# A decoder layer on one core: memory queries and two branch products as seven quarter products each

## The chip, the cores and the metric

One core of a Trainium2 chip runs the whole kernel. The metric is the device time in microseconds of one launch, the median of several runs. Products run on TensorE (PE), element-wise work on VectorE (DVE) and ScalarE (ACT); SyncE (SP) and GpSimd (POOL) issue the transfers. Inputs lie in the chip's memory (HBM), operands in on-chip memory (SBUF), sums of products in eight banks of PSUM.

## The reference

A decoder layer over 512 tokens of width 1024 in float32. One projection of the normed input gives the queries, keys and values of three attention branches and three gates; the branches are mixed, and a SwiGLU network follows.

```python
u = rms_norm(h, ln_mix_pre[l])
proj = jnp.einsum('bsd,de->bse', u, w_in[l])
qa, ka, va, qb, kb, vb, qm, gl = jnp.split(proj, split_idx, axis=-1)
y_swa = swa_sink_attention(...)          # 8 heads of 64, window of 128
y_sb = stick_breaking_attention(...)     # 8 heads of 64
y_mem = memory_cross_attention(...)      # 4 heads of 128, 256 memory positions
g = jax.nn.sigmoid(gl.reshape(B, S, N_BRANCH, D))
merged = (g[:, :, 0] * jnp.einsum('bse,ed->bsd', y_swa, w_branch_swa[l])
          + g[:, :, 1] * jnp.einsum('bse,ed->bsd', y_sb, w_branch_sb[l])
          + g[:, :, 2] * jnp.einsum('bse,ed->bsd', y_mem, w_branch_mem[l]))
mix = jnp.einsum('bsd,de->bse', merged, w_out[l])
h = h + rms_norm(mix, ln_mix_post[l])
u = rms_norm(h, ln_ffn_pre[l])
a = silu(u @ w_gate[l]) * (u @ w_up[l])
h = h + rms_norm(a @ w_down[l], ln_ffn_post[l])
```

The memory queries `qm` are 512 x 1024 by 1024 x 512. Each branch product is 512 x 512 by 512 x 1024.

## The kernel before, in words

Every float32 operand of a large product is split into a high and a low half (`split`: ScalarE rounds the high half, VectorE subtracts it for the low one), and `mm3` makes three products of them: high by high, high by low, low by high. A product works on a stationary block of 128 x 128 and a moving block of 128 rows by up to 512 columns.

The work is a stream of units (class `Stream`). Each unit loads 1024 columns of weights for each of the 128 partitions (512 KB), splits them, and makes its products; loads run four units ahead, splits three. Attention heads (`sb_head`, `swa_pair`, `mem_pair`) are written as steps between which the stream runs for a given number of microseconds (`dn.run`), so that TensorE has stream products while the other engines do the heads' softmax or scan.

The units in order: projections (`proj`), values, memory keys and values, three of the four memory-query projections, the stick-breaking branch (`add_branch(SB)`), the fourth memory query, and then for each branch SB, SWA (local attention) and MEM its gate units, with SWA's and MEM's branch units behind their gates.

- A projection unit for the queries of a memory head (`proj("qm", i)`) has 8 chunks of width 128, each with three products of 512 columns. The result is scaled by the norm of the row and split.
- A branch (`branch_t`) takes two units per half of the output columns. For each of 4 token tiles it multiplies 4 pieces of `y` by the weights, then gates: one multiplication by the gate, one addition to the sum of the branches so far.
- The gates are made as seven quarter products in place of eight, a Strassen scheme (Winograd's form): the input is cut into token halves and chunk halves, the weights into chunk halves and output halves. `QUART` names the seven products p1, p2, p5, p3, p6, p7, p4; each has two units. p1, p6, p7 and p4 add up in one PSUM bank, p5 and p3 in a second, p2 is a third (`QBANK`), and copies taken between them (`q_end`) are joined to the four quarters. Sums of weight quarters are made by loads that add into the buffer of an earlier product (`q_issue`: p1 to p5 to p6 to p4, p3 to p7), on POOL's queue; each such load has to follow the split of what was in the buffer. The sums of input quarters are `qsum`. The feed-forward products have the same form (`gu`, `down`).

`merge` transposes the gated sum of one half of the columns, for all tokens, and splits it; `mix_mm` multiplies it by `w_out`. At the end of the mixing phase the calls stand as: first half of tile 0, `merge(1)`, first half of tile 1, second half of tile 0, and so on.

The order of instructions on each engine is written out in a table (`ORDER`), and the buffer that each tile takes in another (`PLAN`; kinds are raw weights, high and low halves, PSUM banks `p`, the 73 SBUF blocks `ck`, small tiles `s`).

Of the kernel before, what the change touches and what calls it, by code (L numbers as in the profile page):

```python
# [17 lines left out]
P = 128  # L18
# [11 lines left out]
QM_FIRST = 3  # L30
# [11 lines left out]
    ),  # L42
    "vector": (
# [30 lines left out]
    ),  # L74
    "scalar": (
# [24 lines left out]
    ),  # L100
    "gpsimd": (
        "5-12 4 2-3 16 0 29 1 14 13 15 30 17 22 27 21 20 19 18 23 28 25 24 26 31-34 36-37 35 38 40 39 41-49 51 50 "
        "52-65 70 66 69 71 67-68 72-95 107-112 96-99 103 101 100 102 104-106"
    ),
    "sync": (
# [1799 lines left out]
```

## Time and profile before

| | |
|---|---|
| median of 3 runs | 783.92 us (783.35 to 784.14) |
| profiled execution, first to last instruction | 782.6 us |
| TensorE busy | 775.0 us, 99%, 4638 products |
| VectorE busy | 601.9 us, 77% |
| ScalarE busy | 472.9 us, 60% |
| GpSimd busy | 88.5 us, 11% |
| granted TensorE clock | 0.997 |
| bytes moved | 128.61 MB, mean 164 GB/s |

The profiled execution is one execution; its own time is given as the span between its first and last instruction, 1.3 us under the median, which counts the whole launch. A group row of the profile reads: line, engine, operation, out<-in, shapes, count | busy us, mean ns of one | idle time before it and who ended it. A timeline row reads: start, duration, engine, line, operation, out<-in, shapes, count. Almost all instructions have the line of one helper, so groups are told apart by tile names.

### The profile page before, as it was taken

The numbers are of one execution on the slowest core, as the hardware profiler recorded it, in microseconds if no ns is written. First come the engines' busy times: TensorE is split into PE (matmuls) and PEld (weight loads), VectorE is DVE, ScalarE is ACT, GpSimd is POOL, SyncE is SP. The second block draws the span as 40 slices with busy tenths as digits, with TensorE's granted clock in tenths as the row PEclk, the third lists the DMA queues.
The fourth block names the chain that finished last, engine by engine and source line by source line (L and its number), as shares of the span: only waits on it lengthen the run. The fifth ranks groups of instructions, "written<-read, shape, count | busy, mean of one in ns | idle before, by whom it ended". The sixth has DMA issues, their size and how long they took to land.

```text
span 782.6 us, 12274 instructions
## 1 busy us (share of the span) xinstructions
PE 775.0 (99%) x4638; PEld 682.9 (87%) x4638; DVE 601.9 (77%) x961; ACT 472.9 (60%) x843; POOL 88.5 (11%) x117
## 2 busy tenths in 40 slices
PE   9999999999999999999999999999999999999996
PEld 6889888778888888888888899999999999888885
DVE  7995787677886657976856699978677878999876
ACT  7652677677486657556644486545555447666753
POOL 2100400001012120011002101000000000216000
PEclk9999999999999999999999999999999999999998
DMA  8444923245559694379569638977777652959702
GB/s 302 129 142 121 315 90 109 81 126 143 109 118 205 166 189 131 82 190 231 210 240 282 110 105 225 235 190 189 183 182 183 180 159 78 198 128 195 216 1 108
DMA packets 44220, 128.61 MB, mean 164 GB/s; under 512 B 5248, under 2 KB 6832, under 8 KB 44160
## 3 DMA queue, kind: packets, MB, share of 16 engines
q1 hardware_dynamic: 30480, 85.21, 33.4%
q0 software_dynamic: 13248, 42.22, 29.0%
q8 instruction: 36, 0.59, 0.3%
q10 hardware_dynamic: 432, 0.39, 0.2%
q14 instruction: 24, 0.20, 0.1%
HBM read 120.98 MB, written 4.72 MB: 161 GB/s over the span
## 4 chain that ended last, share of the span: by engine, by line
PE 99%; DVE 0%; issue 0%; DVEq 0%; ACT 0%
PE p L185 99%; DVE fg L185 0%; DVEq L1893 0%; DVE s L185 0%; DVE wide L185 0%; ACT sqr L185 0%; DVE eps_t L185 0%
## 5 line engine op out<-in xcount | busy, mean ns | idle before, releaser
L185 DVE TENSOR_TENSOR lo<-raw,hi 128x1024 fp32r<-128x1024 f32 (+4 forms) x139 | 159.4, 1154 | 65.5 <-ACT hi L185 64.8
L185 ACT CAST hi<-raw 128x1024 fp32r<-128x1024 f32 (+4 forms) x139 | 137.5, 997 | 96.3 <-PE p L185 60.0
L185 DVE TENSOR_TENSOR lo<-wide,hi 128x1024 fp32r<-128x1024 f32 x53 | 64.8, 1224 | 22.5 <-ACT hi L185 21.9
L185 ACT CAST hi<-wide 128x1024 fp32r<-128x1024 f32 x53 | 55.6, 1052 | 38.6 <-PE p L185 17.8
L185 PE MATMUL p<-lo,lh 128*128 128x512 f32 x154 | 59.9, 389 | 0.0
L185 PE MATMUL p<-hi,ll 128*128 128x512 f32 x154 | 59.7, 389 | 0.0
L185 PE MATMUL p<-hi,lh 128*128 128x512 f32 x154 | 59.3, 389 | 0.0
L185 PE MATMUL p<-lo,uh 128*128 128x512 f32 (+1 forms) x160 | 57.1, 357 | 0.0
L185 PE MATMUL p<-hi,ul 128*128 128x512 f32 (+1 forms) x160 | 57.1, 357 | 0.0
L185 PE MATMUL p<-hi,uh 128*128 128x512 f32 (+1 forms) x160 | 56.9, 358 | 0.0
L185 PE MATMUL p<-uh,hi 128*128 128x512 f32 x136 | 55.3, 406 | 0.0
L185 PE MATMUL p<-uh,lo 128*128 128x512 f32 x136 | 53.3, 392 | 0.0
L185 PE MATMUL p<-ul,hi 128*128 128x512 f32 x136 | 53.2, 392 | 0.0
L185 POOL DMA_DIRECT2D wide<-in_w_gu x21 | 18.1, 876 | 186.1 <-DMA wide<-in_w_gu 185.7
L185 POOL DMA_DIRECT2D raw<-in_w_g x24 | 20.7, 861 | 135.8 <-DVE lo L185 128.8
L185 PEld LDWEIGHTS p<-lo,lh 128*128 128x128 f32 x154 | 28.9, 188 | 6.0
L185 PEld LDWEIGHTS p<-hi,lh 128*128 128x128 f32 x154 | 28.9, 188 | 6.0
L185 PEld LDWEIGHTS p<-hi,ll 128*128 128x128 f32 x154 | 28.9, 188 | 5.9
L185 PEld LDWEIGHTS p<-hi,uh 128*128 128x128 f32 x160 | 30.0, 188 | 4.0 <-issue 0.2
L185 PEld LDWEIGHTS p<-lo,uh 128*128 128x128 f32 x160 | 30.0, 188 | 3.7
L185 PEld LDWEIGHTS p<-hi,ul 128*128 128x128 f32 x160 | 30.0, 188 | 3.7
L185 ACT COPY gp<-p 128x512 f32<-128x512 f32 x33 | 19.3, 587 | 21.4 <-PE p L185 21.3
(645 smaller groups left out, 2390.0 us busy)
## 6 DMA issues: line engine op xcount, KB each, us to landing
wide<-in_w_gu SPq DMA_DIRECT2D x31, 512.0 KB, 5.1
raw<-in_w_gu SPq DMA_DIRECT2D x26, 512.0 KB, 5.3
raw<-in_w_g POOLq DMA_DIRECT2D x24, 512.0 KB, 5.9
wide<-in_w_gu POOLq DMA_DIRECT2D x21, 512.0 KB, 7.1
raw<-in_w_g SPq DMA_DIRECT2D x18, 512.0 KB, 4.4
raw<-in_w_p SPq DMA_DIRECT2D x14, 512.0 KB, 4.3
raw<-in_w_brt SPq DMA_DIRECT2D x12, 512.0 KB, 4.2
bp<-in_w_dn SPq DMA_DIRECT2D x22, 256.0 KB, 6.9
```

The costliest lines, as they stand in the source:

```text
L185: ins = f(*args, **kw)
```

## The change

Three products take the form that the gates have.

- **Memory queries.** The four `proj("qm", ...)` units go. Seven units `qm_quart` come, each with 2 heads x 4 chunks, three products of 256 columns (half of the tokens). They use the gates' sums of input quarters, so the result is not yet scaled by the row's norm; that scale goes into the softmax of the memory heads (`qscale`).
- **Branches SWA and MEM.** Their four units each go. Seven units `b_quart` come, each with 2 token tiles x 2 pieces, three products of 512 columns. `pair_out` keeps a plain copy of `y` (`yraw`), `y_sums` builds the sums of its quarters, `y_parts` splits them, `c_end` joins the banks and hands each finished tile to gating. For SWA the addition of the SB part becomes an adding transfer on POOL's queue.
- **Weights** of these units: p1, p2, p3 are plain loads by SP, p5, p6, p4 and p7 adding loads by POOL (`c_issue`), issued three units ahead of the earlier product's turn.
- **Order of units.** Query units alternate with the last two gate units of SB and the first five of SWA; SWA's branch units with the last four gate units of SWA, MEM's with the last four of MEM (`woven`).
- **Merging** goes by half of the columns and half of the tokens; the first tile is mixed in one go.
- **Tables.** `ORDER` and `PLAN` are new throughout, the opening and the feed-forward part included. Raw weights may take three further buffers inside the wide block (`kind in ("raw", "fraw") and n > 3`). In the list of PSUM banks the long run of the feed-forward units was `3 5 7 0 2 6 4 1 7 5 3 6 ...` and is `2 2 2 5 5 5 2 2 2 5 5 5 ...`.

```diff
-    def merge(h):
+    CHAIN = {"p5": "p1", "p6": "p5", "p4": "p6", "p7": "p3"}
+    def c_issue(b, p):
+        if p in CHAIN:
+            t = cw[(b, p)] = cw.pop((b, CHAIN[p]))
+            nc.gpsimd.dma_start(t[:, :].rearrange("p (c n) -> p c n", c=2), c_src(b, p), accum_op=ALU.add)
+            return
+        uid[0] += 1
+        t = cw[(b, p)] = places.take(wp, "raw", [P, 1024], F32, f"raw{uid[0]}")
+        nc.sync.dma_start(t[:, :].rearrange("p (c n) -> p c n", c=2), c_src(b, p))
+    def y_sums(b, k):
...
+        nc.vector.tensor_tensor(p5, ya[:, hi], yb[:, hi], op=ALU.subtract)
+        nc.vector.tensor_tensor(p6, p5, ya[:, lo], op=ALU.subtract)
+        nc.vector.tensor_tensor(p3, p6, yb[:, lo], op=ALU.add)
+        nc.vector.tensor_tensor(p7, ya[:, lo], ya[:, hi], op=ALU.subtract)
+    def c_end(b, p, i, put):
+        ps = cbank[(b, QBANK[p], i)]
+        if p in ("p1", "p5", "p6", "p7"):
+            t = ckeep[(b, p, i)] = ck(f"cq{b}{p}{i}")
+            nc.scalar.copy(t[:, :], ps[:, :])
+        if p == "p2":
+            t = ckeep.pop((b, "p1", i))
+            nc.vector.tensor_tensor(t[:, :], ps[:, :], t[:, :], op=ALU.add)
+            put(0, 0, t)
...
+        elif p == "p4":
+            put(1, 0, ps)
+    def b_quart(b, p):
+        def gen(hi, lo):
+            first = p in ("p1", "p5", "p2")
+            for i in range(2):
+                def put(half, h, v):
+                    t = 2 * half + i
+                    g = gate_t[(b, t, h)]
+                    nc.vector.tensor_tensor(g[:, :], v[:, :], g[:, :], op=ALU.mult)
+                    more = acc_t[(t, h)] if b == SWA else gate_t[(SWA, t, h)]
+                    if b == SWA:
+                        nc.gpsimd.dma_start(g[:, :], more[:, :], accum_op=ALU.add)
+                    else:
+                        nc.vector.tensor_tensor(g[:, :], g[:, :], more[:, :], op=ALU.add)
...
+                for k in range(2):
+                    mm3_behind(ps[:, :], b_left(b, p, k, i * P), cols((hi, lo), k * 512, 512), first and k == 0, k == 1)
+                yield 1.36
+                c_end(b, p, i, put)
+            if b == MEM and p in ("p3", "p7"):
+                merge(("p3", "p7").index(p), 0)
+    def qm_quart(p):
...
+            for f in range(2):
+                for k in range(4):
+                    x = q_left(p, k // 2, k % 2, 0, 256)
+                    w = cols((hi, lo), f * 512 + k * P, P)
+                    mm3(ps[:, f * 256 : (f + 1) * 256], w, x, first and f == 0 and k == 0, k == 3)
+                yield 1.44
+    sb, swa, mem = (gate_units(b) for b in (SB, SWA, MEM))
+    seq = sb[:12] + woven(branch_units("qm"), sb[12:] + swa[:5]) + swa[5:10]
+    seq += woven(branch_units(SWA), swa[10:])
+    seq += mem[:10] + woven(branch_units(MEM), mem[10:])
...
-        yield 3.0
+        yield 4.0
...
-    mix_mm(0, 0, 4)
-    merge(1)
-    mix_mm(1, 0, 4)
-    mix_mm(0, 4, KC)
+    mix_mm(0, 0, KC)
+    merge(1, 1)
     tmp[0] = mix(0)
-    mix_mm(1, 4, KC)
+    merge(0, 1)
+    mix_mm(1, 0, KC)
```

More of the change, by code (lines that the diff above doesn't have):

```diff
@@ L241, in take @@
             return pool.tile(shape, dt, tag=f"ck{n}", name=name, bufs=1)
-        if kind == "fraw" and n > 3:
+        if kind in ("raw", "fraw") and n > 3:
             return self.held["wide0"][:, (n - 4) * 1024 : (n - 3) * 1024]
@@ L652, in mem_vals @@
         return gen
-    merged = [None] * 8
+    merged = {}
     QUART = ("p1", "p2", "p5", "p3", "p6", "p7", "p4")
@@ L794, in gen @@
                 for k in range(2):
-                    mm3_behind(qbank[key][:, :], q_left(p, c, k, i), cols((hi, lo), k * 512, 512), first and k == 0, c == 1 and k == 1)
+                    mm3_behind(qbank[key][:, :], q_left(p, c, k, i * P), cols((hi, lo), k * 512, 512), first and k == 0, c == 1 and k == 1)
                 yield 1.36
@@ L810, in gen @@
                 tok = slice(t * P, (t + 1) * P)
-                ps = (aps if b == SB and t % 2 else dps)(f"br{b}{t}{h}")
+                ps = (aps if t % 2 else dps)(f"br{b}{t}{h}")
                 for k in range(4):
@@ L816, in gen @@
                     yield 0.68
-                if b == SB:
-                    acc_t[(t, h)] = ck(f"bs{t}{h}")
-                    with tc.high_priority():
-                        nc.vector.tensor_copy(acc_t[(t, h)][:, :], ps[:, :])
-                    continue
-                g = gate_t[(b, t, h)]
-                with tc.high_priority():
-                    nc.vector.tensor_tensor(g[:, :], ps[:, :], g[:, :], op=ALU.mult)
-                eng = nc.vector
-                more = acc_t[(t, h)] if b == SWA else gate_t[(SWA, t, h)]
@@ L827, in gen @@
-                eng.tensor_tensor(g[:, :], g[:, :], more[:, :], op=ALU.add)
-                if (b, h, t) == (MEM, 1, 1):
-                    merge(0)
-        return gen
-    def merge(h):
-        for c in range(4):
-            pt = (dps if (h, c) in ((1, 0), (1, 1)) else aps)(f"mg{h}{c}")
-            for t in range(NT):
-                nc.tensor.transpose(
-                    pt[:, t * P : (t + 1) * P], gate_t[(MEM, t, h)][:, c * P : (c + 1) * P], ident[:, :]
-                )
-            mh, ml = ck(f"mgh{h}{c}", F32R), ck(f"mgl{h}{c}", F32R)
-            split(pt[:, :], mh[:, :], ml[:, :])
-            merged[4 * h + c] = (mh, ml)
+                acc_t[(t, h)] = ck(f"bs{t}{h}")
@@ new lines, in c_got, with got @@
+    def c_got(b, p):
+        def got():
+            if p not in CHAIN:
+                c_issue(b, p)
+            return cw[(b, p)]
+        return got
+    def y_sums(b, k):
+        lo, hi = slice(0, 256), slice(256, 512)
+        sl = slice(k * 256, (k + 1) * 256)
+        ya, yb = yraw[(b, k)], yraw[(b, 2 + k)]
+        if k == 0:
+            for p in ("p5", "p6", "p3", "p7"):
+                ysum[(b, p)] = ck(f"ys{b}{p}")
+        p5, p6, p3, p7 = (ysum[(b, p)][:, sl] for p in ("p5", "p6", "p3", "p7"))
+        nc.vector.tensor_tensor(p5, ya[:, hi], yb[:, hi], op=ALU.subtract)
+        nc.vector.tensor_tensor(p6, p5, ya[:, lo], op=ALU.subtract)
+        nc.vector.tensor_tensor(p3, p6, yb[:, lo], op=ALU.add)
+        nc.vector.tensor_tensor(p7, ya[:, lo], ya[:, hi], op=ALU.subtract)
@@ new lines, in y_parts, with b_left @@
+    def y_parts(b, p):
+        ysum[(b, p)] = parts(f"yp{b}{p}", ysum[(b, p)])
+    def b_left(b, p, k, o):
+        if p in ("p1", "p2", "p4"):
+            return cols(y[(b, k if p == "p1" else 2 + k)], o + (256 if p == "p4" else 0), P)
+        return cols(ysum[(b, p)], k * 256 + o, P)
+    def c_end(b, p, i, put):
[7 more added lines that the diff above has]
+            put(0, 0, t)
+        elif p == "p6":
+            t = ckeep.pop((b, "p6", i))
+            nc.vector.tensor_tensor(t[:, :], cbank[(b, "y", i)][:, :], t[:, :], op=ALU.subtract)
+            put(0, 1, t)
+        elif p == "p7":
+            t, x = ckeep.pop((b, "p5", i)), ckeep.pop((b, "p7", i))
+            nc.vector.tensor_tensor(t[:, :], t[:, :], x[:, :], op=ALU.subtract)
+            put(1, 1, t)
+        elif p == "p4":
+            put(1, 0, ps)
@@ new lines, in b_quart @@
+    def b_quart(b, p):
[11 more added lines that the diff above has]
+                        nc.vector.tensor_tensor(g[:, :], g[:, :], more[:, :], op=ALU.add)
+                if first:
+                    cbank[(b, QBANK[p], i)] = (dps if p == "p2" else aps)(f"b{b}{p}{i}")
+                ps = cbank[(b, QBANK[p], i)]
+                for k in range(2):
[4 more added lines that the diff above has]
+                merge(("p3", "p7").index(p), 0)
+        return gen
@@ new lines, in qm_quart, with gen, put @@
+    def qm_quart(p):
+        def gen(hi, lo):
+            first = p in ("p1", "p5", "p2")
+            if first:
+                cbank[("qm", QBANK[p], 0)] = (dps if p == "p2" else aps)(f"q{p}")
+            ps = cbank[("qm", QBANK[p], 0)]
+            for f in range(2):
[4 more added lines that the diff above has]
+                yield 1.44
+            def put(half, h, v):
+                st[("qm", h, half)] = parts(f"qms{half}{h}", v)
+            c_end("qm", p, 0, put)
+        return gen
@@ new lines, in merge @@
+    def merge(h, half):
+        for c in range(2):
+            pt = aps(f"mg{h}{c}{half}")
+            for k in range(2):
+                for t in range(2):
+                    o = (2 * c + k) * P
+                    nc.tensor.transpose(
+                        pt[:, (2 * k + t) * P : (2 * k + t + 1) * P],
+                        gate_t[(MEM, 2 * half + t, h)][:, o : o + P],
+                        ident[:, :],
+                    )
+            merged[(h, c, half)] = parts(f"mg{h}{c}{half}", pt)
@@ L845, in tile_kernel, with merged_at @@
+    def merged_at(k, t):
+        return cols(merged[(k // 4, k % 4 // 2, t // 2)], (k % 2) * 256 + (t % 2) * P, P)
     for c in range(8):
@@ new lines, in add_quarters @@
+    def add_quarters(seq):
+        at = {}
+        for kind, b, p, c in seq:
+            at[(kind, b, p, c)] = len(dn.units)
+            if kind == "gate":
+                dn.add(q_got(b, p, c), 1024, quart(b, p, c))
+            else:
+                dn.add(c_got(b, p), 1024, qm_quart(p) if b == "qm" else b_quart(b, p))
+        for kind, b, p, c in seq:
+            if p in CHAIN:
+                u_begin = dn.units[at[(kind, b, CHAIN[p], c)] - (2 if kind == "gate" else 3)]["begin"]
+                if kind == "gate":
+                    u_begin.append(lambda b=b, p=p, c=c: q_issue(b, p, c))
+                else:
+                    u_begin.append(lambda b=b, p=p: c_issue(b, p))
+            if kind == "branch" and b != "qm":
+                n = at[(kind, b, p, c)]
+                if p == "p1":
+                    for k in range(2):
+                        dn.units[n - 2 + k]["begin"].append(lambda b=b, k=k: y_sums(b, k))
+                elif p not in ("p2", "p4"):
+                    dn.units[n - 2]["begin"].append(lambda b=b, p=p: y_parts(b, p))
+        return at
@@ new lines, in gate_units, with branch_units, woven @@
+    def gate_units(b, ps=QUART):
+        return [("gate", b, p, c) for p in ps for c in range(2)]
+    def branch_units(b, ps=QUART):
+        return [("branch", b, p, 0) for p in ps]
+    def woven(*rows):
+        out = []
+        rows = [list(r) for r in rows]
+        while any(rows):
+            for r in rows:
+                out += r[:1]
+                del r[:1]
+        return out
+    sb, swa, mem = (gate_units(b) for b in (SB, SWA, MEM))
+    seq = sb[:12] + woven(branch_units("qm"), sb[12:] + swa[:5]) + swa[5:10]
@@ new lines, in tile_kernel @@
+    seq += woven(branch_units(SWA), swa[10:])
+    seq += mem[:10] + woven(branch_units(MEM), mem[10:])
+    g0 = len(dn.units)
+    at = add_quarters(seq)
+    dn.units[at[("gate", SWA, "p4", 1)]]["flags"].append(f"gates{SWA}")
+    dn.units[at[("gate", MEM, "p2", 1)]]["flags"].append("gates_late")
+    dn.mark(f"branch{MEM}")
+    for g, what, f, args in (
+            (-8, "begin", x_quarters, (1, 1)),
+            (-8, "begin", x_quarters, (0, 1)),
+            (-7, "begin", x_quarters, (0, 0)),
+            (-6, "begin", x_quarters, (1, 0)),
+            (-6, "begin", q_sum1, (0,)),
+            (-5, "begin", q_sum1, (1,)),
+            (-4, "begin", q_sum2, ()),
+            (-3, "begin", q_gain, (1,)),
+            (-2, "begin", q_sum3, ()),
+            (-1, "begin", q_gain, (0,)),
+            (0, "begin", q_sum4, ()),
+            (1, "begin", q_parts, ("p5", 0)),
+            (2, "begin", q_parts, ("p5", 1)),
+            (3, "begin", q_parts, ("p3", 0)),
+            (4, "begin", q_parts, ("p3", 1)),
+            (5, "begin", q_parts, ("p6", 0)),
+            (6, "begin", q_parts, ("p6", 1)),
+            (7, "begin", q_parts, ("p7", 0)),
+            (8, "begin", q_parts, ("p7", 1)),
+        ):
+            dn.units[g0 + g][what].append(lambda f=f, args=args: f(*args))
@@ L1061, in pair_out @@
     def pair_out(b, c, ps):
+        if b != SB:
+            yraw[(b, c)] = ck(f"yr{b}{c}")
+            nc.scalar.copy(yraw[(b, c)][:, :], ps[:, :])
         y[(b, c)] = parts(f"y{b}{c}", ps)
@@ L1222, in mem_pair @@
                 )
-            nc.vector.tensor_scalar(nm, nm, -MS, None, op0=ALU.mult)
+            nc.vector.tensor_tensor(nm, nm, qscale[:, 4:], op=ALU.mult)
             for n in range(NT):
                 fn(
-                    blocks(w[h], n), blocks(s[h], n), AF.Exp, bias=nm[:, n : n + 1], scale=MS, accum_out=den[:, n : n + 1]
+                    blocks(w[h], n),
+                    blocks(s[h], n),
+                    AF.Exp,
+                    bias=nm[:, n : n + 1],
+                    scale=qscale[:, n : n + 1],
+                    accum_out=den[:, n : n + 1],
                 )
@@ L1320, in mix_mm @@
     def mix_mm(t, k0, k1):
-        tok = slice(t * P, (t + 1) * P)
         if k0 == 0:
```

96 lines of the change are left out of this document (31 added, 65 removed), and 183 rows, old and new, of tables (ORDER, PLAN).

## The prediction

> **What bounds the kernel now.** I read the page first: busy times, then the chain that ended last, then the list of waits of TensorE alone.
>
> ```profile
> span 782.6 us, 12274 instructions
> PE 775.0 (99%) x4638; PEld 682.9 (87%) x4638; DVE 601.9 (77%) x961; ACT 472.9 (60%) x843; POOL 88.5 (11%) x117
> PE 99%; DVE 0%; issue 0%; DVEq 0%; ACT 0%
> PE p L185 <- DVE wide L185: 1.4, 1, 1.4
> ```
>
> TensorE is busy for 99% of the span, the chain runs along it, and its only listed wait is 1.4 us at the start. So the kernel is as long as its list of products, each at the pace at which products follow one another. That pace is not the "mean ns of one" of a group, since neighbours overlap; it is the distance between starts:
>
> ```profile
> 308.00 0.39 PE L185 MATMUL p<-hi,y00h 128*128 128x512 f32 x1
> 310.72 0.39 PE L185 MATMUL p<-hi,y00h 128*128 128x512 f32 x1
> 561.98 0.28 PE L185 MATMUL p<-T3h,hi 128*128 128x256 f32 x1
> 564.86 0.28 PE L185 MATMUL p<-B21h,hi 128*128 128x256 f32 x1
> 51.73 0.31 PE L185 MATMUL p<-hi,uh 128*128 128x320 f32 x1
> 52.17 0.31 PE L185 MATMUL p<-hi,uh 128*128 128x320 f32 x1
> ```
>
> The first two are the same product of two token tiles, 12 products apart: 2.72/12 = 0.2267 us for 512 columns. The next two are 24 products apart: 2.88/24 = 0.1200 us for 256 columns. The last two, three apart, give 0.147 us for 320 columns.
>
> **The change part by part: TensorE.** These rows show the products that are replaced:
>
> ```profile
> L185 PE MATMUL p<-uh,hi 128*128 128x512 f32 x136 | 55.3, 406 | 0.0
> L185 PE MATMUL p<-hi,y10h 128*128 128x512 f32 x8 | 3.1, 390 | 0.0
> ```
>
> A projection unit is 8 chunks times 3 products (hi by hi, hi by lo, lo by hi), so 136 is 17 units, 4 of them memory queries. They go: 4 x 24 = 96 products, 96 x 0.2267 = 21.76 us. In come 7 quarters x 2 heads x 4 chunks x 3 = 168 products of 256 columns, 168 x 0.1200 = 20.16 us. Gain 1.60 us.
> In a branch, each left piece (y10h and so on) meets 2 halves x 4 tiles = 8 times; 4 pieces x 8 x 3 = 96 products. After: 7 x 2 x 2 x 3 = 84, of the same 512 columns. Gain 12 x 0.2267 = 2.72 us for local attention, the same for memory, 5.44 us.
> The transposes of the merge stay 32, the scores of the memory heads stay as they are. Together **-7.04 us** of TensorE.
>
> **VectorE.** Its pace, too, is the distance of starts:
>
> ```profile
> 386.70 0.69 DVE L185 TENSOR_TENSOR wo14l<-wo,wo14h 128x512 fp32r<-128x512 f32 x1
> 387.31 0.69 DVE L185 TENSOR_TENSOR wo05l<-wo,wo05h 128x512 fp32r<-128x512 f32 x1
> 569.72 1.23 DVE L185 TENSOR_TENSOR lo<-raw,hi 128x1024 fp32r<-128x1024 f32 x1 [0.23 <-ACT hi L185]
> 570.86 0.42 DVE L185 TENSOR_TENSOR aq<-gp,sg 128x256 f32<-128x256 f32 x1
> 571.20 1.22 DVE L185 TENSOR_TENSOR raw<-raw,raw 128x1024 f32<-128x1024 f32 x1
> ```
>
> That is 0.61 us for 512 elements, 1.14 for 1024, 0.34 for 256. The memory branch adds 3 splits of weights (3.4), 8 sums of y quarters (2.7), 4 splits of these sums (2.4) and 6 joins of banks (3.7): +12.2 us. Local attention adds the same and gives its 8 adds (4.9) to DMAs: +7.3. The queries add 3 splits and lose one evacuation net: +2.8. In all +22.3, so 624 of some 775 us, 81%. On average that is cover enough; in the last stretch it is not plenty. Where that stretch lies today, and the fullest stretches elsewhere:
>
> ```profile
> 300.00:342.00 42.00, 42.00 (x226) 36.17 (x225) 36.03 (x67) 24.98 (x57) 1.72 (x2) 1.00 0.37 93
> 342.00:404.00 62.00, 62.00 (x284) 51.54 (x283) 43.55 (x57) 35.73 (x53) 5.16 (x6) 1.00 0.77 214
> 342.00:382.00 40.00, 40.00 (x179) 33.10 (x178) 25.97 (x30) 29.18 (x42) 5.16 (x6) 1.00 0.94 252
> 448.00:476.00 28.00, 28.00 (x235) 27.88 (x234) 26.88 (x49) 21.88 (x46) 1.72 (x2) 1.00 0.44 111
> 672.00:756.00 84.00, 84.00 (x373) 69.53 (x372) 75.68 (x119) 56.74 (x96) 17.47 (x21) 1.00 0.71 161
> ```
>
> Columns: stretch, PE, PEld, DVE, ACT and POOL busy, clock, DMA share, GB/s. From 300 to 404 us (both branches, memory heads, memory gates) VectorE works 79.6 of 104 us. After, the same work needs 79.6 + 12.2 + 7.3, and the four last units of the local gates are woven in (4 splits and 2 joins, 5.8): **105 us of VectorE work beside 104 - 5.4 + 4 x 2.72 = 109.4 us of products, 96%**. At 448 to 476 us VectorE is at 26.88/28 = 96% and TensorE lost nothing; at 672 to 756 it is at 90% for 84 us, again without loss. So it can be covered, with nothing to spare. The scaling of the memory maxima changes its operand, not its count.
>
> **ScalarE** gets 45 instructions more (9 splits, 20 copies out of PSUM, 8 splits of sums, 8 copies of y):
>
> ```profile
> L185 ACT CAST hi<-raw 128x1024 fp32r<-128x1024 f32 x120 | 125.5, 1053 | 85.1 <-PE p L185 54.8 <-DVE raw L185 16.7 <-issue 8.6
> L185 ACT COPY gp<-p 128x512 f32<-128x512 f32 x33 | 19.3, 587 | 21.4 <-PE p L185 21.3
> ```
>
> At most 9 x 1.05 + 36 x 0.6 = 31 us, 504 of 775: hidden, since today it idles 40%.
>
> **DMA.** SP issues 3 loads fewer (3 x 3 raw quarters for 3 x 4 halves); POOL issues 12 accumulating loads and 8 adds of 256 KB more, on the queue that also carries the gates' accumulations.
>
> ```profile
> q1 hardware_dynamic: 30480, 85.21, 33.4%
> q0 software_dynamic: 13248, 42.22, 29.0%
> raw<-in_w_g POOLq DMA_DIRECT2D x24, 512.0 KB, 5.9
> xq<-xq POOLq DMA_DIRECT2D x8, 256.0 KB, 5.3
> DMA to landing us min/median/max: 2.6/5.2/17.1
> ```
>
> By the first two rows 512 KB take 1.61 us of all 16 engines on q1 (33.4% of 782.6 over 85.21 MB) and 2.82 on q0. So +12 x 2.82 + 8 x 1.41 - 3 x 1.61 = +40 us. For the stretch above: 0.37 x 42 + 0.77 x 62 = 63 today; plus two branches (2 x 9.7), the adds (11.3) and four gate units (9.2) makes 103 of 109 us, 94%. The row 342 to 382 shows that share for 40 us, TensorE full. A quarter's chain is split, add, split, add, split, add, split in one buffer. From the first split to the products of p4 it has 13 units x 2.72 = 35.4 us; it needs 4 x (1.05 + 1.23) + 3 x 5.9 = 26.8. So landings may grow from 5.9 to 8.7 us before TensorE waits. I cost it at nothing. The 8 adds of local attention are wanted only by the memory branch's adds, some ten gate units later. All of them stand in POOL's queue in order: an accumulation that waits for its split holds up what is behind it, another chain's accumulation or an add. Two small scalings on POOL for the queries' scale stand there too:
>
> ```profile
> L185 POOL TENSOR_SCALAR wide<-wide 128x8 f32<-128x8 f32 x1 | 0.2, 250 | 0.1
> ```
>
> 0.5 us, wanted only by the memory heads: nothing.
>
> **The tables.** PSUM is laid out anew. Today the feed-forward units rotate through eight banks; the new table, as I read its list, gives them two, 2 and 5, so the first product of a unit's second sum follows into the bank that p4 just left. Today p4 starts and is read out here:
>
> ```profile
> 567.74 0.28 PE L185 MATMUL p<-T4h,hi 128*128 128x256 f32 x1
> 572.33 0.42 DVE L185 SCALAR_TENSOR_TENSOR aq<-p,sg 128x256 f32<-128x256 f32 x1
> ```
>
> p4 ends 2.88 us after its start, at 570.62; its bank is free at 572.75, 2.13 later, with 2.88 us of p1 in between. Covered, by 0.75 us. Without that cover each of some ten units would pay what is missing. The opening is reordered as well:
>
> ```profile
> 5.24 0.99 PE L185 MATMUL p<-uh,hi 128*128 128x512 f32 x1
> 7.76 0.40 PE L185 MATMUL p<-uh,hi 128*128 128x512 f32 x1
> ```
>
> Six products take 2.52 us for 1.36, so 1.2 us could be won there at most; I bound it by 1.2 either way and take 0. At the end of mixing, the first tile's 48 products (10.9 us) now stand between the last gating (p4) and the merges of the second token half: cover for its 4 mults and adds (2.4 us) and 4 splits.
>
> **The sum.** -7.04, plus new waits of TensorE between 0 (the two rows at 96% and 94%) and 6.9 (VectorE at the 90% of 672 to 756: 105/0.90 - 109.4 = 7.3, less what the mixing can take over). The nearest rows in load show no loss but are 28 and 40 us long, not 109; I take **+1.0**. The profiled span is 782.6, the median 783.92, 1.3 more for what lies outside: span 776.6, time 783.92 - 6.04 = **777.9**.
>
> **The rivals.**
> *VectorE becomes the bound (slower).* One mechanism: joins, gatings and sums queue ahead of the lo splits in the woven stretches, so TensorE waits for weights. It decides where VectorE can be filled to less than about 0.90: then 105/0.90 - 109.4 = 7 eats the gain. At 0.85 it is 123.5 - 109.4 = +14, time 790.9. For: VectorE already waits much for ScalarE's hi halves, and waits can't be filled at will (first row below). Against: the 90 and 96% rows. Chance 0.20, over half of it beyond the point.
>
> ```profile
> DVE lo L185 <- ACT hi L185: 91.2, 122, 4.1
> POOL raw L185 <- DVE lo L185: 136.2, 25, 31.9
> ```
>
> *Accumulating loads land late.* At 10 us per landing a chain lacks 3 x (10 - 8.7) = 3.9 us at p4 of the memory branch, where p6 and p4 stand only two units apart: 783.92 - 6.04 + 3.9 = 781.8. For: 94% of the DMA engines, a 17.1 us maximum, and the second row: POOL's accumulations already wait for splits, which a full VectorE makes later. Against: the median 5.9. Chance 0.11.
> The Trainium skill (SBUF — State Buffer, Who interferes with whom) says that VectorE and GpSimd share a port pair under an exclusive lock, so that descriptors of POOL's DMAs can be held up. The rows here do not bear that out for these forms:
>
> ```profile
> 344.50 0.86 POOL L185 DMA_DIRECT2D raw<-in_w_g  x1 [12.32 <-DVE lo L185]
> 358.54 0.86 POOL L185 DMA_DIRECT2D raw<-in_w_g  x1 [5.02 <-DVE lo L185]
> 358.76 2.35 DVE L185 TENSOR_TENSOR lo<-raw,hi 128x1024 fp32r<-128x1024 f32 x2
> ```
>
> The second issue runs under a two-operand VectorE instruction and takes the same 0.86 us.
> *Narrow products don't pay.* At more than 21.76/168 = 0.1295 us the queries lose; at the 0.147 of 320 columns they cost 24.7, and the time is 783.92 - 5.44 + 2.9 + 1.0 = 782.4. Against: the 0.1200 row, the same form. Chance 0.03.
> The Trainium skill (TensorE: Matmul & The Clock Gate, Back-to-back issue gap) gives 81 ns a product at 128 columns and 131 at 512 sustained; on a straight line an estimate of 98 at 256 would make the queries lose 3.9 us, the branches gain 3.1, the time 784.7. This trace disagrees: 0.2267 us at 512.
>
> **How the numbers follow.** Forecast 776 to 780: 0.66. The late landings and narrow products still end faster: with them 0.80. Of VectorE's 0.20, 0.09 within 0.2% (1.6 us, about what a measurement here can tell from no change) and 0.11 slower. The range runs from the full gain with 1.2 us won in the opening (783.92 - 8.24 = 775.7) up to 784.5, past the point where the gain is eaten; what lies above is about 0.1.
>
> **What would show it.** Right: no 256-column group dearer than 0.12 us between starts; 84 products per branch; no TensorE wait over 0.5 us from 10 us on; VectorE over 90% beside the last woven units. Wrong: TensorE waiting for VectorE's lo, or for a raw buffer of the branch weights at p7 or p4; or waits on PSUM at each feed-forward unit, which would be the tables' doing.

## The result and the profile after

The changed kernel takes **809.67 us** (median of 4 runs, 807.75 to 811.91) against 783.68 us beside it: ratio 1.0332, 95% interval 1.0313 to 1.0350. The prediction was 777.9 us; the sign is wrong. The page of the changed kernel, the lines that answer to the first ones shown of before:

```profile
span 807.9 us, 12635 instructions
PE 776.7 (96%) x4686; PEld 680.9 (84%) x4686; DVE 618.3 (77%) x997; ACT 547.2 (68%) x926; POOL 110.0 (14%) x139
PE 42%; ACT 6%; DVE 2%; issue 1%; DVEq 0%; ACTq 0%
```

ScalarE works 74.3 us more (472.9 to 547.2) where 31 were expected, and the chain that ended last, before all of TensorE, now runs over ScalarE and VectorE too. TensorE's list of waits, one line long before:

```profile
PE p L186 <- DVE mt L186: 7.3, 4, 3.5
PE p L186 <- ACT mw L186: 3.0, 3, 1.8
PE p L186 <- ACT B11h L186: 2.3, 1, 2.3
PE p L186 <- ACT hi L186: 1.5, 1, 1.5
```

The names `mt` and `B11h` belong to the mixing and to the norm behind it, where the change alters only the order of merging. (`mw` are the exponentials of a memory head, `hi` the high half of a weight.) Where the time went is seen with busy times by stretch (columns as in the prediction), of before:

```profile
200.00:404.00 204.00, 204.00 (x986) 170.03 (x985) 150.29 (x240) 125.24 (x218) 22.39 (x26) 1.00 0.67 161
404.00:490.00 86.00, 86.00 (x563) 78.69 (x562) 64.46 (x122) 52.56 (x116) 11.21 (x13) 1.00 0.76 200
490.00:680.00 190.00, 190.00 (x1552) 188.53 (x1551) 150.03 (x183) 104.70 (x150) 17.20 (x20) 1.00 0.69 175
```

and of after:

```profile
200.00:404.00 204.00, 196.59 (x1001) 162.73 (x1000) 156.01 (x258) 158.92 (x268) 37.92 (x42) 0.99 0.86 196
404.00:490.00 86.00, 76.36 (x432) 65.77 (x431) 57.45 (x119) 62.20 (x116) 8.63 (x10) 0.98 0.53 128
490.00:680.00 190.00, 190.00 (x1586) 190.00 (x1585) 148.41 (x179) 99.03 (x142) 14.65 (x17) 1.00 0.73 194
```

From 490 to 680 us (feed-forward) TensorE is full in both. It stands idle for 7.4 us in the woven stretch (200 to 404 us) and 9.6 in the mixing (404 to 490 us), both 0 before; from 680 us to the end of the span it is 11.3 against 6.3. What fills ScalarE is one group, on the page of after

```profile
L186 ACT ACT_TABLE_LOAD x47 | 60.3, 1283 | 7.0 <-DVE s L186 4.1 <-issue 2.1
```

and in before's list of groups

```profile
L185 ACT ACT_TABLE_LOAD x9 | 11.5, 1283 | 2.3 <-issue 2.1
```

A load of ScalarE's function table takes 1.283 us; 38 more are 48.8 us. ScalarE's timeline in the mixing of after (start, duration, engine, line, operation):

```profile
429.88 1.28 ACT L186 ACT_TABLE_LOAD   x1
431.18 0.29 ACT L186 ACTIVATE s<-s,s 128x1 f32<-128x1 f32 x1
...
432.43 1.28 ACT L186 ACT_TABLE_LOAD   x1
433.72 0.20 ACT L186 ACTIVATE s<-s 128x1 f32<-128x1 f32 x1
...
435.90 1.28 ACT L186 ACT_TABLE_LOAD   x1 [1.40 <-DVE s L186]
```

The two `s` rows are the logarithm and the exponential of one norm (`rsqrt`): each brings its own load. Behind its first load the program asks for eight changes of table (`preload_act_table_set`), four of them to `natural_log_exp_and_others`, which serves both functions. In the new `ORDER["scalar"]` these eight stand ahead of the last functions of the table before. In the trace a further load then stands ahead of the old function, and from there on one at every change between logarithm and exponential. The trace does not show what puts these loads in.

### The profile page after: what moved, and what is told of

It reads as the page before. It is cut to its first block, busy times and chain, and to the rows that moved or that the text cites. A ratio compares the mean times of both kernels' runs of the same rounds, so it can differ in the third digit from the quotient of the medians.

```text
span 807.9 us, 12635 instructions
## 1 busy us (share of the span) xinstructions
PE 776.7 (96%) x4686; PEld 680.9 (84%) x4686; DVE 618.3 (77%) x997; ACT 547.2 (68%) x926; POOL 110.0 (14%) x139
## 4 chain that ended last, share of the span: by engine, by line
PE 42%; ACT 6%; DVE 2%; issue 1%; DVEq 0%; ACTq 0%
PE p L186 42%; ACT L186 3%; ACT mt L186 1%; DVE mt L186 1%; ACT s L186 1%; DVE s L186 0%; ACT hi L186 0%; DVE fg L186 0%; DVE xr L186 0%; DVE mg011l L186 0%; ACT sqr L186 0%; DVEq L2045 0%; ACT B11h L186 0%; ACT mg011h L186 0%; ACT mg001h L186 0%
## 5 line engine op out<-in xcount | busy, mean ns | idle before, releaser
L186 DVE TENSOR_TENSOR lo<-raw,hi 128x1024 fp32r<-128x1024 f32 (+5 forms) x118 | 134.0, 1138 | 41.4 <-ACT hi L186 40.6
L186 ACT CAST hi<-raw 128x1024 fp32r<-128x1024 f32 (+5 forms) x118 | 116.2, 986 | 71.8 <-PE p L186 56.4
L186 ACT CAST hi<-wide 128x1024 fp32r<-128x1024 f32 x83 | 87.2, 1052 | 83.9 <-PE p L186 50.2
L186 DVE TENSOR_TENSOR lo<-wide,hi 128x1024 fp32r<-128x1024 f32 x83 | 101.4, 1223 | 39.9 <-ACT hi L186 39.6
L186 PE MATMUL p<-uh,hi 128*128 128x512 f32 (+1 forms) x136 | 50.9, 375 | 1.4 <-ACT uh L186 0.9
L186 PE MATMUL p<-uh,lo 128*128 128x512 f32 (+1 forms) x136 | 49.6, 365 | 0.0
L186 PE MATMUL p<-ul,hi 128*128 128x512 f32 (+1 forms) x136 | 49.6, 366 | 0.0
L186 POOL DMA_DIRECT2D raw<-in_w_gu x17 | 14.6, 861 | 148.5 <-DMA raw<-in_w_gu 148.1
L186 DVE TENSOR_TENSOR_SCAN bw<-br,bw 128x512 f32<-128x512 f32 (+3 forms) x32 | 23.9, 804 | 10.3 <-ACT bw L186 10.3
```

Of the source, the lines that this page charges most:

```text
L186: ins = f(*args, **kw)
```

## The experiments

**Put the loads back (e1).** Eight numbers of `ORDER["scalar"]` move behind the last function of the old table (and one sigmoid behind the exponentials); 9 loads remain. One of the eight (455 is the last sigmoid, 471 the load for the norms):

```diff
-454 456 438 471 437 442-443 ... 459 470 455 453 460-461
+454 456 438 437 442-443 ... 459 470 455 471 453 460-461
```

> The changed kernel, only the written-out order of ScalarE touched: each of the eight explicit loads of an activation table stands behind the last function of the old table and before the first of the new one (one sigmoid moves behind the exponentials it stood among). 9 table loads in place of 46. Theory A (misplaced table loads cost the whole loss, and the seven-product form is worth about its 7.0 us): mixing back to 83.9 us from its first product to the first T4 product, the tail behind the last product back to 6.3 us, the stretch before mixing up to 7 us shorter than before; time 777 to 780. Theory B (VectorE or the accumulating loads bound the woven stretches, table loads cost only mixing and tail): 809.7 - 17.5 - 5.1 = 787, no better. Theory C (the two PSUM banks of the feed-forward units): above 800, nothing regained there.

Measured 791.46 us (790.55 to 793.03), 1.0095 [1.0080, 1.0110]: 18.2 us below after, 7.3 above before. No theory's number (777 to 780, 787, above 800): the loads are most of the loss, not all.

**Half of them (e2, e3).** e2 moves only the last three loads (mixing and tail, 20 loads remain), e3 only the five earlier ones (36 remain in the trace, not the 35 expected).

> The changed kernel with only the last three explicit table loads put right (before mixing, before the feed-forward part, before the down products); 20 table loads. A and B alike: mixing -17.5 us and tail -5.1 us against the changed kernel: 787. A: the nine to ten us still missing lie before mixing and go in the first run of this set; B: they stay there too.

> The changed kernel with only the first five explicit table loads put right; 35 table loads, mixing and tail as in the changed kernel. A: the stretch before mixing gains 7 to 9 us, time 801 to 803. B: it gains under 3 us, time 807 to 810.

Measured 794.52 us (1.0135 [1.0119, 1.0150]) and 807.92 us (1.0306 [1.0283, 1.0329]). The late loads cost 15.2 us of the 18.2. The early ones cost 1.8 by themselves, where the intervals overlap, and 3.1 once the late ones are right. e3 falls where B put it; e2 is 7.5 us above what both theories gave. With the late loads right TensorE idles 0.9 us in the mixing, and its waits for `mt` are gone: there a norm waits for its own loads, and TensorE for the norm. In the woven stretch TensorE's idle time hardly moves, 7.4 us in after and 7.2 in e3.

**The same fault in the kernel before (e4).** Every load of before's table moves ahead of the last function of the old table; 46 loads in the trace, not the 38 expected. For the load ahead of the norms:

```diff
-467-470 483 481 488 482 479 494
+467-469 479 470 483 481 488 482 494
```

> The kernel before, only ScalarE's order touched: each explicit table load moved ahead of the last function that needs the old table; 38 table loads in place of 9. A: the same loss in mixing and tail without any of the new products: +20 to +25 us, 804 to 809. B: mixing and tail as in A (+22), as B blames the loads there too. C: no change, 784.

Measured 800.75 us, 1.0213 [1.0196, 1.0230]. The group of loads in its trace:

```profile
L183 ACT ACT_TABLE_LOAD x46 | 59.0, 1283 | 2.8 <-issue 2.1
```

That is 17 us for 37 more loads, without the change, a little less than the 20 to 25 expected. TensorE idles 8.9 us from 404 to 490 us, as in after, but only 0.4 from 200 to 404. So the loads are shown as a cause from both sides.

**What is left in e1: ScalarE's order (e5).** TensorE's waits in e1, and one of them in the timelines of ScalarE and TensorE:

```profile
PE p L185 <- ACT hi L185: 2.1, 1, 2.1
PE p L185 <- ACT cq2p L185: 1.8, 2, 0.9
PE p L185 <- DVE wide L185: 1.4, 1, 1.4
PE p L185 <- ACT mw L185: 1.1, 2, 0.6
```

```profile
218.45 1.28 ACT L185 ACT_TABLE_LOAD   x1
219.74 0.72 ACT L185 ACTIVATE gq1p<-gq1p,wide 128x512 f32<-128x512 f32 x1
220.37 1.03 ACT L185 CAST hi<-raw 128x1024 fp32r<-128x1024 f32 x1
...
221.45 0.50 PE L185 MATMUL p<-hi,xsp60h 128*128 128x512 f32 x1 [2.09 <-ACT hi L185]
```

A needed load and a sigmoid stand ahead of the cast that TensorE needs first. (`cq...` is a copy of a quarter product out of PSUM, `gq...` a gate.) None of these waits is for a `lo` of VectorE. e5 moves these and some others, with one swap on VectorE in the opening:

```diff
-... 265-266 282-283 269 271-273 284 ...    (282: sigmoid load)
+... 265-266 269 271-273 282-283 284 ...
-0-4 6 5 8          455 471 453 460         393 408 402 398-399 409 403 410 400-401
+0-6 8              473 471 476             402 398-399 403 400-401 408-410   (also 360)
```

> The kernel with its table loads put right (791.5 us), with five further moves in ScalarE's order and one in VectorE's, no instruction added or taken away: the sigmoid table's load at 218.45 us and the first sigmoid go behind the four casts and copies that TensorE's next products wait for; the natural-log table's load at 399.0 goes behind the casts and copies up to the first logarithm; the sigmoid load at 351.56 goes behind the casts mpts20h to mpts31h; the load at 318.74 goes behind two weight casts; and in the opening the first cast of x goes ahead of the second weight cast. Theory A (what is left of the loss is ScalarE's queue, served late at a few places): the wait of 2.24 us at 218.98 with the drop of the granted clock to 0.91 behind it (about 2 us), the wait of 1.02 us at 400.6, 0.5 us at 356 and 0.95 us in the opening come back: 785 to 787.5. Theory B (VectorE bounds the stretch from 200 to 404 us): no instruction of VectorE changes but one swap in the opening: 790 to 792. Theory C (the transfers' contention slows the products): 790 to 792.

Measured 789.38 us, 1.0067 [1.0053, 1.0081]. The wait at 219 us went, yet only 2.1 us were won, between what A and what B and C gave. TensorE's list of e5 has the wait for `mw` grown and a new one:

```profile
PE p L184 <- ACT mw L184: 2.5, 3, 1.5
PE p L184 <- ACT gq2p L184: 1.8, 1, 1.8
```

**Load either engine (e6, e7).** Both double the same 20 copies, on one engine or the other:

```diff
             nc.scalar.copy(t[:, :], ps[:, :])
+            nc.scalar.copy(t[:, :], t[:, :])         # e6
+            nc.vector.tensor_copy(t[:, :], t[:, :])  # e7
```

> The kernel e5, with each of the 20 copies of a quarter product out of PSUM (cq...) followed on ScalarE by a copy of the tile onto itself (128x512): about 20 x 0.49 us = 9.8 us more on ScalarE between 220 and 404 us, nothing more on VectorE. Theory A (ScalarE's queue is what TensorE waits for there): 3 to 8 us above e5. Theory B (VectorE bounds): 0 to 2 us above e5.

> The kernel e5, with the same 20 tiles copied onto themselves on VectorE instead, each right before the sum or difference that takes the tile: 20 x 0.4 to 0.7 us = 8 to 14 us more on VectorE between 220 and 404 us, nothing more on ScalarE. Theory A: 0 to 3 us above e5, less than e6. Theory B (VectorE bounds): 8 to 14 us above e5, more than e6.

Measured 794.07 us (1.0130 [1.0115, 1.0146]) and 795.20 us (1.0143 [1.0125, 1.0161]): +4.7 us for 12.1 us more of busy time on ScalarE (498.4 to 510.5), +5.8 for 7.4 more on VectorE (617.3 to 624.7). Both theories fall, since each spares one engine. About 40% of what is added to ScalarE and 80% of what is added to VectorE ends up in the time.

**A further order, and room (e8 to e11).** e8 moves casts that wait for transfers behind work that is ready; e9 to e11 keep e8's order and cut the work:

```diff
-364 370 365 ...   462-463 447 445          473 471 476
+364 356 370 365   462-463 445 447          466 471 492        (e8; also 360, 408, 409, 410)
...
+            nh, nl = (128, n) if short else (n, n)      # e9; e10: (n, 128); e11: (128, 128)
+            ins = nc.scalar.copy(hi[:, :nh], raw[:, :nh])
+            lows = nc.vector.tensor_tensor(lo[:, :nl], raw[:, :nl], hi[:, :nl].bitcast(F32), op=ALU.subtract)
```

> The kernel e5 with ScalarE's order changed at four places more: the cast of the weights that an accumulating load brings (idle 1.62 us at 316 us, 2.23 us at 391.7 us, both times behind that load) goes behind the four exponentials and behind the copy cq2p that TensorE waited for, and the sigmoid load at 352 us and the natural-log load at 417.7 us go to places where ScalarE is free. Theory A (ScalarE's queue alone): the waits 1.45 + 0.59 us (mw), 1.77 us (gq2p), 1.20 us (cq2p) and 1.46 us at 415.9, with the lower clock behind the first (about 1.5 us), go: 789.4 - 7 = 781 to 784. Theory D (ScalarE and VectorE are both so full in the woven stretch that a wait taken away at one place comes back at the next): 786 to 789.

> The kernel e8, with the 21 casts (ScalarE) of the weights of the 21 quarter products of queries and branches cut from 1024 columns to 128; the rest of those weights is left as it stands in the buffer, so the products there are of other numbers. VectorE's 21 subtractions stay whole. ScalarE has about 21 x 0.74 = 15.5 us less between 200 and 404 us. Theory A: 4 to 8 us below e8. Theory D: 2 to 4 us below e8, part of it only. Theory B (VectorE bounds): 0 to 1 us.

> The kernel e8, with the 21 subtractions (VectorE) of the same weights cut from 1024 columns to 128, the casts whole; the rest of the low halves is left as it stands in the buffer. VectorE has about 21 x 0.9 = 19 us less. Theory A: 0 to 1 us below e8. Theory D: 2 to 4 us below e8. Theory B: 6 to 10 us below e8.

> The kernel e8, with both the casts and the subtractions of those 21 weights cut to 128 columns: 15.5 us less on ScalarE and 19 us less on VectorE; what is not split is left as it stands in the buffer. Theory D: 6 to 9 us below e8, near the 778 of the prediction, the engines having about the room they had before. Theory A: as e9. Theory B: as e10. Theory C (transfers and their contention, which stay whole here): no more than 2 us below e8.

Measured 787.91 us (1.0051 [1.0038, 1.0065]), 786.45 (1.0033 [1.0020, 1.0045]), 787.20 (1.0042 [1.0028, 1.0056]) and 786.04 (1.0036 [1.0023, 1.0049]). The intervals overlap: 15 us less on ScalarE and 18 on VectorE, together, bring at most 2 to 3 us. Of the forecasts for e11 only C's holds, that of the transfers. Adding work hurts, taking it away hardly helps, so something else must hold some of the waits.

**Late accumulating transfers (e12 to e14).** In e8 ScalarE stands at the head of its queue for one of them, with the exponentials of a memory head behind it, and TensorE waits for those:

```profile
346.10 0.62 ACT L184 CAST wo11h<-wo 128x512 fp32r<-128x512 f32 x1 [2.10 <-DMA gq0p<-bs]
346.63 0.56 ACT L184 ACTIVATE mw<-p,s,wide 128x256 f32<-128x256 f32 x1
...
350.13 0.30 PE L184 MATMUL p<-c_ident,mw 128*128 128x128 f32 x1 [1.85 <-DVE mw L184]
```

The cast has nothing to do with the gate: in `PLAN` its result takes SBUF block 15, which held `bs20`, the source of such a transfer, so it must wait until the transfer has read it. (`wo00l`, below in e16, takes block 47 of `bs30` in the same way.) e12 makes the transfers plain, e13 moves this cast (419) behind the exponentials, e14 gives the eight sums of gates back to VectorE.

```diff
-            nc.gpsimd.dma_start(..., c_src(b, p), accum_op=ALU.add)
+            nc.gpsimd.dma_start(..., c_src(b, p))                                    # e12
-                        nc.gpsimd.dma_start(g[:, :], more[:, :], accum_op=ALU.add)
+                        nc.gpsimd.dma_start(g[:, :], more[:, :])                     # e12
+                        nc.vector.tensor_tensor(g[:, :], g[:, :], more[:, :], op=ALU.add)  # e14
-418-419 386-389 397 390-393 402     364 356 370 365-368 371
+418 386-389 397 390-393 419 402     364 370 356 365-366 371 367-368                  # e13
```

> The kernel e8, with the 12 weight loads and the 8 additions of gates that the change does by accumulating transfers made plain transfers on the same queue, of the same size, at the same places of the order; the sums are left out, so the products are of other numbers. Theory E (accumulating transfers land late, 7.0 us for the weights and 9.4 us for the gates where plain loads of SyncE take 4.2 to 4.7, and hold the head of ScalarE's queue): they land in 4 to 6 us, ScalarE's waits for them of 2.10 and 0.54 us and TensorE's wait of 1.9 us at 348 go, and the time is 3 to 5 us below e8: 783 to 785. Theory A (ScalarE's order alone) and theory D (no room on the engines): within 1 us of e8.

> The kernel e8 with three more moves on ScalarE: the cast wo11h, which stood idle 2.10 us for an accumulating transfer, goes behind the eight exponentials queued behind it, and two copies cq0p go ahead of the cast and the two exponentials that stood before them. Theory E and theory A: TensorE's waits of 1.9 us (mw) and 1.7 us (cq0p) and the lower clock behind the first go: 783 to 785. Theory D: they come back at the next place: 787 to 788.

> The kernel e13, with the eight sums of gate and block branch done by VectorE (as the kernel before does them) in place of eight accumulating transfers: 8 x 0.68 = 5.4 us more on VectorE and eight transfers of 256 KB fewer. Theory E: 1 to 3 us below e13. Theory D and B (VectorE has no room): 2 to 4 us above e13.

Measured 786.05 us (1.0030 [1.0018, 1.0041]), 787.01 (1.0049 [1.0035, 1.0062]) and 790.83 (1.0090 [1.0076, 1.0103]). The median times to landing in e8 and then in e12 (count, KB each, us):

```profile
wide<-in_w_brt POOLq DMA_DIRECT2D x7, 512.0 KB, 7.0
gq0p<-bs POOLq DMA_DIRECT2D x8, 256.0 KB, 9.4
```

```profile
wide<-in_w_brt POOLq DMA_DIRECT2D x7, 512.0 KB, 4.7
gq0p<-bs POOLq DMA_DIRECT2D x8, 256.0 KB, 5.9
```

Plain transfers land 2.3 and 3.5 us sooner, and 1.9 us of time go with it, less than the 3 to 5 expected; TensorE's wait of 1.9 us for `mw` is gone. The DMA share from 200 to 404 us falls too, from 0.86 to 0.79, so e12 does not tell late landing from full DMA engines. e13 ends where theory D put it: the waits that it takes away come back elsewhere. Eight more adds on VectorE (5.4 us) cost 3.8 over e13: the transfers are still the better choice.

**Both at once, and the last orders (e15 to e18).** e15 is e8 with e11's and e12's edits together. e16 and e17 go on from e13 with orders alone; e18 is e17 with e15's edits.

```diff
-vector 390 397 386 398 404      scalar 398-399 408-409 403 410 400-401 411
+vector 390 397 398 404 386      scalar 398-399 403 400-401 411 ... 440 408-410 432    (e16; also 372, 412)
-vector 443 428 454 429-432      scalar 404-405 412 425 406-407 413 ... 440 408-410 432
+vector 443 428 429-432 454      scalar 404-405 408 412 425 406-407 409-410 413        (e17)
```

> The kernel e8 with what e11 and e12 do at once: the 21 casts and 21 subtractions cut to 128 columns, and the 20 accumulating transfers made plain; sums and most of the splits of those weights are left out. Theory F (late transfers and full engines each hold the same two places, so that either alone lets the other take over): 3 to 6 us below e8, 782 to 785. Theory G (the rest is the order of the steps on TensorE, which puts products of the attention too soon behind the exponentials that they need): 1.5 to 2.5 us below e8, as e11 and e12 alone.

> The kernel e13 with more moves of order alone: on VectorE the subtraction that waited 3.25 us for a late accumulated weight goes behind the subtraction and the maximum that were ready; on ScalarE the sigmoid table's load at 352 us and its two sigmoids go behind the copies and casts up to 364 us, and a weight cast goes behind two copies cq0p. Theory H (orders that put late work ahead of ready work): TensorE's waits of 1.76 us (lo), 0.72 us (cq0p) and 1.03 us (mpts30h) go: 3 to 4 us below e13, 783 to 784, level with the kernel before. Theory D (no room: the waits come back at the next place): 786 to 787.

> The kernel e16 with two moves: on VectorE the subtraction wo00l, which stood idle 1.50 us for an accumulating transfer, goes behind the four scalings of mw queued behind it; on ScalarE the sigmoid table's load goes into an idle time of 1.5 us at 356 us and its two sigmoids 5 us earlier than in e16. Theory H (orders that put late work ahead of ready work): TensorE's waits of 2.18 us (mw) and 1.93 us (gq2p) go: 784 to 785. Theory D (the waits come back at the next place): 787 to 788.

> The kernel e17 with what e15 does to e8: the 21 casts and the 21 subtractions cut to 128 columns and the 20 accumulating transfers made plain; most of the splits of those weights and the sums are left out. Theory F (late transfers and full engines hold the woven stretch): 3 to 5 us below e17, 782 to 784, a little under the kernel before; the waits of about 2.4 us at 207 to 226 us, where attention stands beside attention on TensorE, stay, and so do about 2 us at 319 to 355 us. Theory G (TensorE's own order is all that is left): within 1 us of e17.

Measured: e15 784.09 us (1.0003 [0.9994, 1.0012]), e16 788.24 (1.0057 [1.0044, 1.0070]), e17 786.75 (1.0046 [1.0032, 1.0060]), e18 **781.57** (0.9973 [0.9962, 0.9984]). e15's 3.8 us below e8 lie in F's range, but they are the sum of e11's 1.9 and e12's 1.9, so they do not show that either hides the other. e17 is near what D gave, e18 a little below F's range. e16 is a miss that shows the mechanism. By 341 us it was 2.6 us ahead of e13, and lost that again behind the next transfer, now on VectorE:

```profile
346.95 0.69 DVE L184 TENSOR_TENSOR wo00l<-wo,wo00h 128x512 fp32r<-128x512 f32 x1 [1.50 <-DMA gq0p<-bs]
347.56 0.61 DVE L184 TENSOR_SCALAR mw<-mw,s 128x256 f32<-128x256 f32 x2
...
348.06 0.87 PE L184 MATMUL p<-c_ident,mw 128*128 128x128 f32 x6 [2.18 <-DVE mw L184]
```

Its other wait, 1.93 us for `gq2p`, stands behind its own late sigmoids; it is 1.2 in e17, which moves them forward. The stretch from 200 to 404 us in e1, e17 and e18, one row of each:

```profile
200.00:404.00 204.00, 197.95 (x1007) 163.91 (x1006) 157.68 (x257) 149.90 (x261) 38.91 (x44) 0.99 0.87 202
```

```profile
200.00:404.00 204.00, 200.32 (x1031) 166.67 (x1030) 161.40 (x264) 150.32 (x263) 40.39 (x45) 1.00 0.87 207
```

```profile
200.00:404.00 204.00, 203.29 (x1051) 170.79 (x1050) 147.56 (x274) 137.17 (x265) 33.45 (x45) 1.00 0.80 216
```

TensorE's idle time there falls from 7.4 us (after) to 6.1, 3.7 and 0.7, and only then is the kernel under before. e18 leaves out more than the change brought (12 of its 21 splits stood in before too), so it is a bound, not a version to use. No kernel that computes the whole layer beat the kernel before; the best is e17, 0.46% slower.

## Why the prediction was wrong

In the order in which the runs took them away, the 31.8 us between 777.9 and 809.67 split into 18.2 us for table loads (809.67 to e1), 4.7 for orders (e1 to e17), and at most 5.2 for full engines and late transfers together (e17 to e18, which leaves out more than the change brought). The other 3.7 stay open. Counted from 783.92 - 7.04 = 776.9, without the 1.0 for new waits, they are 4.7: in e18's profile TensorE idles 2.3 us more than before (0.7 up to 200 us, 0.7 in the woven stretch, 0.9 behind 680 us), its busy time falls by 5.7 (775.0 to 769.3) and not by 7.04, and 2.4 us lie outside the span where the prediction took 1.3.

- **TensorE, -7.04 us: right in count and pace.** The page counts 48 products more (168 - 96 - 24). Two query products of after, 23 apart, give 2.76/23 = 0.1200 us:

```profile
252.91 0.28 PE L186 MATMUL p<-xsp50h,hi 128*128 128x256 f32 x1
...
255.67 0.28 PE L186 MATMUL p<-xsp51h,lo 128*128 128x256 f32 x1
```

  So the rival of narrow products is out.
- **The tables: the step that failed.** "The tables" looked at PSUM banks and the opening and costed both at nothing. That much held: no wait on PSUM in the feed-forward part, and the first product stood at 5.24 us before, 6.19 in e1 and, with two casts swapped (and two instructions of VectorE), 5.43 in e5, inside the 1.2 that I allowed. But `ORDER["scalar"]` also says where ScalarE's table loads stand, and these were never looked up. This term, put at nothing, measured 18.2 us. The row of nine loads was in the profile of before; the check would have been whether each load still follows the last function of the old table.
- **ScalarE, "at most 31 us, hidden, since today it idles 40%": the size was right, the cover not.** Without the extra loads it works 74.3 - 48.8 = 25.5 us more. An engine that works its queue in order and has 27% idle time (149.90 of 204 us in e1) still makes TensorE wait where a load, a late cast or an exponential stands at its head. An average share says nothing on that; the prediction asked the question for VectorE alone.
- **VectorE, 96% from 300 to 404 us: over-sized.** In e1 it worked 83% of that stretch, and over the whole span 15.7 us more than before, not 22.3:

```profile
300.00:404.00 104.00, 100.41 (x475) 81.49 (x474) 86.28 (x135) 82.94 (x143) 21.06 (x25) 1.00 0.92 230
```

  The rival that it becomes the bound is not shown: TensorE's waits in e1 behind the opening are for ScalarE but for 0.2 us, and 18 us less work bring under 1 us (e10). But it has no slack where it counts: 5.4 us more cost 3.8 (e14).
- **Accumulating loads: the rival (0.11) was real, its place wrong.** The prediction took 5.9 us to land, with room to 8.7; the weights took 7.0 and the gates' adds 9.4. In the waits followed here no chain was late at p4; what waited for these transfers stood ahead of other work in ScalarE's and VectorE's queues. e12 prices them at 1.9 us alone, e15 and e18 at 3.8 and 5.2 together with room on the engines.
- **New waits, +1.0: mis-sized.** With the loads right (e1) they are 791.5 - 776.9 = 14.6 us, twice the 6.9 that I bounded them by.

TensorE's own order is not tested either. In e17 and e18 alike small waits remain at 207 to 226 us, where attention products follow one another, 0.7 and 0.6 us in all; no run changed that order.

## What to carry to other kernels

A table of instruction orders is code: when it is drawn up anew, look up in it every instruction that sets a state, above all the loads of ScalarE's function tables, and count them in the trace first. When a change takes time from the engine that bounds and gives work to the others, their average idle time does not pay for it; ask, for each in-order queue, what stands ahead of the instruction that the bounding engine needs next, and put work that waits for a transfer behind work that is ready. Waits taken away one by one come back at the next late thing: e16 won and lost the same 2.6 us.

## What the runs showed of the hardware

- **Loads of function tables.** The Trainium skill (ScalarE: Activation LUTs, Table sets: the hidden batching unit) counts one load for a logarithm and an exponential behind it, since one set holds both. The kernel before and e1 agree (9 loads); after does not, with a load for each of the two and 47 in all. In these runs that page's rule to batch calls by set paid only where the load that is asked for stood behind the last call of the old set.
- **The clock after a short wait.** In e5 TensorE waited 1.45 and 0.59 us, and the products behind followed at 0.43 us in place of 0.23 for some 3 us. By stretch, and in TensorE's timeline:

```profile
320.00:340.00 20.00, 18.03 (x80) 14.59 (x81) 17.37 (x32) 14.63 (x33) 7.83 (x9) 0.91 0.90 201
```

```profile
321.38 0.50 PE L184 MATMUL p<-hi,uh 128*128 128x512 f32 x1 [1.45 <-ACT mw L184]
322.47 0.50 PE L184 MATMUL p<-hi,uh 128*128 128x512 f32 x1 [0.59 <-ACT mw L184]
...
323.54 0.63 PE L184 MATMUL p<-lo,yp0p7h 128*128 128x512 f32 x1
323.97 0.63 PE L184 MATMUL p<-hi,yp0p7l 128*128 128x512 f32 x1
```

  The granted clock of that stretch is 0.91, 9% of 20 us, so a wait of 2 us cost about 4. It is not so behind every such wait: behind e16's 2.18 us the granted clock from 340 to 360 us is 1.00, behind e8's 1.85 and 0.58 in the same stretch 0.91.
- **Accumulating transfers** took 7.0 and 9.4 us to land where plain ones of the same size, queue and place took 4.7 and 5.9.
